# A new order table for all engines of a decoder layer: weight sums and loads at other places, the same instructions

## The chip, the core and the metric

The kernel runs on one core of one Trainium2 chip. Its time is the device time of the program in microseconds (us), the median of several runs.

## The reference

One post-norm hybrid decoder layer on 512 tokens of width 1024, all in float32. A combined input projection feeds two mixers: an attention with three branches (compressed blocks, selected blocks, sliding window) and a gated DeltaNet (a short convolution, a decay per head, a chunked recurrence). The two results are merged with gates and projected; then comes a gated MLP of width 2816 with a convolution of width 3 between the up-projection and the activation.

```python
h = x @ w_in
y_a = nsa_attention(...) @ w_nsa_out
y_b = gated_deltanet(...) @ w_gdn_out
mix = (sigmoid(gate_a) * y_a + sigmoid(gate_b) * y_b) @ w_o
x = layer_norm(ALPHA * x + mix, ln1_g, ln1_b)
f = conv_ffn(x, ffn_w_up, ffn_conv_w, ffn_w_down)   # up, conv, silu(gate) * val, down
x = layer_norm(ALPHA * x + f, ln2_g, ln2_b)
```

## The kernel before

**Arithmetic.** TensorE works on float32 values that are cut into two halves: a cast makes the high half, a subtraction from the original the low half. For weights, `split_w` loads a raw tile by a DMA on SP's queue (three buffers `raw`), ACT casts it to `wh` (L424, three buffers) and DVE subtracts to get `wl` (L428, three buffers), each for one half of the tile at a time. `product` then runs three matmuls per slice of the contraction: high by high (L438), high by low (L440) and low by high (L441), 24 matmuls for the 8 slices of a width of 1024.

**Stages.** By the profile's clock: the input projection and the mixers up to some 340 us; the merge with its gates (tiles `pm` and `gps`) to about 425; the output projection (`o_product`, L1243, with its loads in `o_load`, L1126 to L1130) and the first layer norm (L1188 to L1208) to about 475; the up-projection to about 735; the down-projection (L1407) to about 847; at the end the second layer norm and the stores.

The up-projection has 22 pairs p of a gate block and a value block. A pair is two products in two PSUM tiles `pu`; ACT scales one tap of the convolution (L1362), DVE adds the other two (L1365), ACT takes the tanh, and Pool (GpSimd) multiplies gate and value (`fth`, L1371). ACT casts this to `ph` and DVE makes the low half and the sums of blocks that the down-projection needs. Each engine executes its instructions in their order, so ACT's casts of activations (`ph`) and of weights (`wh`, L424) stand in one line.

**Sums of weights.** The output projection and the down-projection are each done with 7 products of blocks in place of 8, as in Strassen's scheme. That needs sums of weight blocks, which are made in DRAM by Pool's DMA queue, partly with accumulation: four tiles `osum` (L458, 8 DMAs of 1024 KB) and four tiles `wsum` (L468, 8 DMAs of 2816 KB). `wsum` is made by `sums(n, after)` in the up-projection, at the pairs in `ROUNDS`; two of its DMAs copy an earlier sum into a new tile before more is added:

```python
todo = [[(0, w_block(0, 0), 0), (1, w_block(0, 1), 0)], [(0, w_block(0, 1), 1)], [(1, w_block(1, 1), 1)],
        [(2, wsum[1], 0)], [(2, w_block(0, 0), 1)], [(3, wsum[2], 0)], [(3, w_block(1, 0), 1)]][n]
for to, src, add in todo:
    i = G.dma_start(out=wsum[to], in_=src, **({"accum_op": OP.add} if add else {}))
```

The down-projection's `block` (L1331 to L1343) and `o_load` read these sums as they read the weights themselves.

**Decays.** Near the start DVE makes the decay factors of the DeltaNet: `gdec` (L576), 16 values a row, then two halves of it, and PE multiplies it by three constant matrices into `dps` (L582). At the same time ACT, Pool and DVE work on the taps of the short convolution (L598 on Pool, L600 on DVE).

**The order.** `body` emits all instructions; then `queues()` chains the instructions of each engine in an order written out by hand in the table `QUEUES`. A number there is the place of an instruction in the order in which the engine's instructions were emitted, and the engine executes them in the order of the table. It holds 3880 numbers for PE, 1275 for DVE, 799 for ACT, 172 for Pool and 185 for SP. The numbers that matter below:

- Pool: 104 to 111 are the eight DMAs of `osum`. 140 and 141 are the copies that begin `wsum0` and `wsum1`; 144 and 147 add to them; 150 copies `wsum1` to `wsum2` and 153 adds to it; 157 copies `wsum2` to `wsum3` and 160 adds to it. 112 and those after are the small works of merge, first norm and up-projection, among them the 22 products `fth`. 3 is the addition of a tap of the convolution.
- SP: 76 loads the rows of the first layer norm (`ln1`, L1188), 77 to 80 are the loads of x, 81 to 89 loads of the output projection, 90 to 93 the first loads of the up-projection (`raw<-in_up`), 135 loads the rows of the second norm.
- DVE: 54 is `gdec`, 74 a tap of the convolution (L600); 833 is the first statistic of the first norm (L1250), 876 the subtraction for the first weights of the up-projection (L1301).
- PE: 2558 to 3790 is most of the up-projection and the down-projection.

```python
for n in range(int(a), int(b or a) + 1):
    i = made[k][n]
    if last is not None:
        tc.add_manual_dep(i, last.name, mybir.DependencyInfo(
            mybir.DependencyClass.NoSync, mybir.DependencyReason.SCHED_ONLY), reason="place in its queue")
    last = i
```

Of the kernel before, what the change touches and what calls it, by code (L numbers as in the profile page):

```python
# [14 lines left out]
OP = mybir.AluOpType  # L15
# [5 lines left out]
KD = 8  # L21
# [49 lines left out]
def layout(a):  # L71
# [58 lines left out]
SUMS = [4, 5, 2, 3, 8, 9, 10, 22]  # L130
# [4 lines left out]
    "PE": """0-9 11-12 10 13-39 47 40-43 53 44-45 54 50 46 48-49 59 51 60 55-56 52 57-58 61 65 62 66 63-64 74 71 75 67-69 72-73  # L135
77-78 83 76 79 84 86-87 85 70 95 89-91 80-81 107 88 108 98 82 109-112 99 92 101 96 113-118 102 97 93 103 119-120 94
121-123 100 124-149 155-172 150 173-178 151-154 104-106 183-204 207 205-206 208-230 235-236 179-181 237 182 238-247
259 248-249 260 250-252 261-262 253 263 254-255 231 264 256 265-267 232-234 257 268-269 302 270 258 271 303 272-277
304 278 305 279-281 306 282 307 360-361 308-311 283-298 362-363 388 364-367 389 368-371 390 372-377 391 378 312-313
379 392 380-382 393 383 394 299-301 314-315 395-410 416 411 444 417-418 445-446 419-433 456 434 457-458 435 459 436  # L140
447 437 460-462 448-449 463 438-439 464-471 450 472-474 451 316 320 317-318 321 319 322-323 475-477 324-327 513 478
514 328 332-334 329-331 335-339 515 479 516 340-347 517-518 348-355 519-520 356-359 384-387 521-524 412-413 525-527
414 528-529 415 530-532 440-443 533 723-730 480-481 452 534 484 482-483 731-732 485 501-502 733 535 734 486 453 735
487 536 736 503 454 488 504 489 737 490 455 738 751 491-492 739-742 493 752 494 743 495 505 507-508 744 506 496-497
753-756 745 509 757-758 541 510 542 759-760 511-512 498 761-762 543 499 763 546 544-545 547 746 764-765 500 766 548
767 560-561 549-551 768-772 552 773 562 774 565 563 553 566 554-555 567-569 537-538 591 539 556-557 592 564 540 581
558 570 582 593-597 559 598-600 796 571 797-799 583-584 800 585 801-802 586 572 803-804 573-574 805-806 575-576
587-589 601 807 602 808-809 577 810-811 590 603-604 578-579 605 812-813 651 606-607 814 652 580 815-816 608-611 653
620 817 621 654 612 818-819 622-626 613-617 864-865 618-619 627 641-642 628-629 866-868 630 869-871 643 872-873
# [12 lines left out]
968 1238 1150 1239 1151 969 1152 1179 1153-1154 1237 970-971 1155 1180 1156-1157 972-973 1181 1158 1182 1240-1241 974
1159 975 1160 976 1161 1183 1162-1164 1184-1189 1242 1190-1193 1243 1194-1199 1025 1137-1140 1026-1027 1200-1201 1283
1028 1284-1285 1202 1244 1286 1252-1253 1287 1307 1165-1168 1308 1245 1169 1309-1310 1170 1311 1254 1257 1312-1314
1246 1258 1247 1255 1259 1171-1173 1260 1174 1256 1315 1175 1316-1317 1261 1176 1248-1249 1262 1177-1178 1273-1274
1318 1288 1319 1250-1251 1275 1277 1289-1290 1263 1278 1291 1264-1267 1276 1320-1322 1268 1323 1279 1403-1404
1269-1271 1229 1324-1325 1280-1281 1272 1326 1282 1327 1230 1292 1328-1329 1405 1330 1406 1293 1407-1408 1231 1294
1409-1413 1295 1232 1296-1298 1422 1299-1302 1414 1303 1423 1415-1416 1424-1425 1417 1426 1418 1427 1379 1428
1304-1305 1380-1382 1419-1420 1383-1385 1429-1430 1386 1431 1443 1432 1444 1387-1392 1445 1331 1421 1306 1447-1448
1433-1434 1446 1435-1437 1449 1438-1440 1393 1441 1453-1454 1450 1332 1442 1394-1395 1455-1456 1396 1458 1451-1452  # L170
1459 1397 1457 1398-1401 1477 1402 1460-1461 1333-1334 1472 1478-1479 1462-1463 1473 1480-1481 1474 1482-1483 1475
1464 1484-1486 1501-1502 1465 1487-1489 1466-1467 1476 1503 1490 1468 1504-1505 1469 1506 1470 1335 1517 1471
1339-1342 1336-1338 1507-1508 1518 1509-1511 1343-1346 1512 1491 1513 1492 1347-1348 1351-1358 1349 1514 1350
1493-1498 1359-1366 1519 1521-1522 1499 1367 1371-1374 1368-1370 1523 1582 1520 1583 1544 1500 1515-1516 1375-1378
1524-1525 1584 1545 1585 1527 1610-1614 1528-1529 1526 1586-1587 1530 1546-1548 1615 1549-1550 1616 1531 1551-1553
1617 1532 1618 1554 1619 1588 1533 1589 1563-1564 1590 1620 1555 1621 1556 1534-1535 1557 1622 1591 1565 1558 1623
1592 1536 1559-1560 1568-1569 1561 1593-1594 1570-1571 1537 1566-1567 1538 1624 1562 1625-1626 1595-1598 1539 1572
1634 1627-1628 1573 1540 1635 1629-1630 1599 1541 1636 1600 1574 1637 1631 1638 1575 1632 1601-1602 1542-1543 1633
1576-1578 1603-1604 1639-1641 1579-1580 1642 1605 1581 1643-1644 1658-1659 1645-1646 1660 1647 1661-1663 1606-1608
1664-1666 1609 1648 1667-1672 1649-1650 1673-1676 1682-1683 1677 1684-1686 1678-1679 1687-1688 1680 1689 1681 1690  # L180
1651-1652 1691-1692 1653 1694 1654 1695 1655 1706 1656 1693 1707 1696 1657 1697-1698 1718-1719 1708 1699 1709 1700
1710-1713 1701-1702 1720-1722 1703 1714-1715 1723 1704 1724 1716 1705 1725-1726 1730-1731 1717 1732 1727 1733
1742-1743 1728 1744 1729 1734 1745 1735 1746-1752 1754 1753 1736 1755 1737-1739 1756 1740 1757-1758 1741 1759-1763
1778 1764-1765 1779-1788 1766-1768 1789 1769 1790 1770 1791 1771-1772 1802 1773 1792 1774 1793 1803-1804 1775-1776
1794-1795 1777 1805 1796 1806 1814 1797-1799 1807 1800 1815-1817 1808 1801 1818-1819 1809 1820 1826 1810 1821-1823
# [125 lines left out]
def body(ctx: ExitStack, tc: tile.TileContext, d, out):  # L311
    nc = tc.nc
    V, A, G, PE = nc.vector, nc.scalar, nc.gpsimd, nc.tensor
# [979 lines left out]
    first = {}  # L1293
# [233 lines left out]
```

## Time and profile before

| | |
|---|---|
| median of 3 runs | 857.27 us (855.77 to 859.29) |
| the profiled execution, time | 855.53 us |
| its span in the trace | 853.7 us |
| mean granted clock of TensorE | 0.983 |
| SP's DMA queue (q1) | 87.37 MB, 28560 packets |
| Pool's DMA queue (q0) | 31.46 MB, 8224 packets |
| DMA in all | 119.57 MB, 140 GB/s in the mean |

The span runs from the first to the last event that the profiler recorded, the time of the execution takes in what lies around it. The granted clock is the share of TensorE's full speed that the throttle allowed. The shares of busy time of the engines stand in the prediction.

### The profile page before, as it was taken

What the parts mean: (1) busy time and instruction counts of PE and PEld (TensorE: products, weight loads), DVE (VectorE), ACT (ScalarE), POOL (GpSimd) and SP (SyncE); (2) the same over time, 40 slices, a digit from 0 to 9 for tenths busy, and PEclk for the clock granted to TensorE, in tenths of its full rate; (3) what the DMA queues carried; (4) which work ended last, traced back from release to release, by engine and by line L of the source; (5) the groups of instructions that cost most, each with busy time, mean ns of one, the idle gap of its engine ahead of it and who ended that gap; (6) DMA issues with size and microseconds to landing.
All of it is one profiled execution on the core that took longest, in us unless ns stands there. A gap on an engine that the chain in (4) does not pass through costs nothing.

```text
span 853.7 us, 11766 instructions
## 1 busy us (share of the span) xinstructions
PE 814.2 (95%) x4138; PEld 674.5 (79%) x4138; DVE 616.5 (72%) x1339; ACT 409.5 (48%) x912; POOL 178.5 (21%) x176
## 2 busy tenths in 40 slices
PE   9799999899999999999998999979689999999996
PEld 8688788778788888888786988868568888887884
DVE  5757779979868965575578948747287777767886
ACT  4434477864567764232353324424144444556541
POOL 0334634232075111331100102122021111100000
PEclk9999999999999999999999999989989999999998
DMA  8423160052114033343266212989897932475662
GB/s 275 137 82 102 51 170 29 25 144 95 60 51 99 26 81 93 124 148 124 76 205 237 75 50 97 349 177 277 196 211 242 225 99 87 135 254 168 200 229 99
DMA packets 36842, 119.57 MB, mean 140 GB/s; under 512 B 3472, under 2 KB 4624, under 8 KB 35600
## 3 DMA queue, kind: packets, MB, share of 16 engines
q1 hardware_dynamic: 28560, 87.37, 31.6%
q0 software_dynamic: 8224, 31.46, 15.5%
q8 instruction: 32, 0.52, 0.2%
q14 instruction: 26, 0.21, 0.1%
HBM read 116.72 MB, written 33.55 MB: 176 GB/s over the span
## 4 chain that ended last, share of the span: by engine, by line
PE 74%; DVE 11%; issue 7%; DMA 4%; ACT 2%; POOL 2%; SPq 0%; DVEq 0%; POOLq 0%; ACTq 0%
PE gps L438 8%; PE gps L440 8%; PE gps L441 8%; PE pu L441 7%; PE pu L438 6%; PE pu L440 6%; PE px L1407 5%; PE pz L1407 3%; PE pout L1044 2%; PE pm L438 2%; PE pm L441 2%; PE pm L440 2%; PE aps L1030 2%; PE dps L614 1%; DVE wl L428 1%
## 5 line engine op out<-in xcount | busy, mean ns | idle before, releaser
L428 DVE TENSOR_TENSOR wl<-raw,wh 128x512 fp32r<-128x512 f32 x146 | 112.8, 774 | 59.6 <-ACT wh L424 46.0
L438 PE MATMUL pu<-mh,wh 128*128 128x512 f32 (+1 forms) x384 | 141.0, 379 | 12.7 <-ACT wh L424 12.7
L441 PE MATMUL pu<-mh,wl 128*128 128x512 f32 (+1 forms) x384 | 141.2, 379 | 1.3 <-DVE wl L428 1.3
L440 PE MATMUL pu<-ml,wh 128*128 128x512 f32 (+1 forms) x384 | 140.8, 377 | 0.0
L424 ACT ACTIVATE wh<-raw 128x512 fp32r<-128x512 f32 x126 | 78.7, 627 | 116.8 <-PE pu L440 79.0
L438 PE MATMUL gps<-xh,wh 128*128 128x512 f32 x320 | 126.8, 406 | 1.8 <-ACT mt L1076 1.8
L441 PE MATMUL gps<-xh,wl 128*128 128x512 f32 x320 | 126.7, 409 | 0.6 <-DVE wl L428 0.6
L440 PE MATMUL gps<-xl,wh 128*128 128x512 f32 x320 | 127.0, 405 | 0.0
L438 PEld LDWEIGHTS pu<-mh,wh 128*128 128x128 f32 x384 | 72.4, 191 | 26.5 <-ACT wh L424 13.6
L441 PEld LDWEIGHTS pu<-mh,wl 128*128 128x128 f32 x384 | 72.7, 191 | 15.3 <-DVE wl L428 2.4
L440 PEld LDWEIGHTS pu<-ml,wh 128*128 128x128 f32 x384 | 72.5, 192 | 13.0 <-DVE ml L1223 0.2
L1365 DVE SCALAR_TENSOR_TENSOR fa<-pu,fcw,fa 128x511 f32<-128x511 f32 (+1 forms) x88 | 65.5, 746 | 12.1 <-ACT fa L1362 10.7
L438 PEld LDWEIGHTS gps<-xh,wh 128*128 128x128 f32 x320 | 60.8, 191 | 12.9 <-issue 2.6
L441 PEld LDWEIGHTS gps<-xh,wl 128*128 128x128 f32 x320 | 60.7, 190 | 11.7 <-DVE wl L428 0.7
L440 PEld LDWEIGHTS gps<-xl,wh 128*128 128x128 f32 x320 | 60.7, 190 | 10.1
L1371 POOL TENSOR_TENSOR fth<-fth,fa 128x512 f32<-128x512 f32 x22 | 32.6, 1484 | 155.0 <-DVE fa L1365 132.9
L1342 ACT ACTIVATE wh<-raw 128x512 fp32r<-128x512 f32 x67 | 40.3, 626 | 40.4 <-DMA raw<-in_down 9.5
L1343 DVE TENSOR_TENSOR wl<-raw,wh 128x512 fp32r<-128x512 f32 x67 | 43.7, 684 | 19.5 <-ACT wh L1342 19.5
L480 POOL TENSOR_TENSOR rs<-rs,minus_half 128x1 f32<-128x1 f32 x8 | 7.2, 899 | 173.9 <-DVE rs L1201 173.9
L428 POOL TENSOR_TENSOR wl<-raw,wh 128x512 fp32r<-128x512 f32 x30 | 39.5, 1320 | 13.8 <-PE gps L441 6.5
L1003 ACT ACTIVATE sc<-sc,mn 128x384 f32<-128x384 f32 (+2 forms) x64 | 35.6, 558 | 13.6 <-DVE mn L1001 12.4
L1030 PE MATMUL aps<-ident,sc 128*128 128x128 f32 x160 | 35.1, 276 | 1.2 <-DVE sc L1014 0.7
(365 smaller groups left out, 1722.8 us busy)
## 6 DMA issues: line engine op xcount, KB each, us to landing
raw<-in_up SPq DMA_DIRECT2D x44, 512.0 KB, 5.4
raw<-in_wT SPq DMA_DIRECT2D x40, 512.0 KB, 3.6
wsum<-in_down POOLq DMA_DIRECT2D x6, 2816.0 KB, 21.8
raw<-wsum SPq DMA_DIRECT2D x20, 512.0 KB, 3.9
raw<-in_down SPq DMA_DIRECT2D x15, 512.0 KB, 4.0
osum<-in_wo POOLq DMA_DIRECT2D x6, 1024.0 KB, 8.4
wsum<-wsum POOLq DMA_DIRECT2D x2, 2816.0 KB, 11.5
raw<-in_wm SPq DMA_DIRECT2D x8, 512.0 KB, 3.8
```

What stands on the lines that cost most here:

```text
L424: A.activation(wh, r, AF.Copy)
L428: eng.tensor_tensor(wl, r, wh.bitcast(F32), op=OP.subtract)
L438: i = PE.matmul(ps, wh[k], mh_(k), start=(k == 0), stop=False)
L440: PE.matmul(ps, wh[k], ml_(k), start=False, stop=False)
L441: PE.matmul(ps, wl[k], mh_(k), start=False, stop=(k == n - 1))
L1003: A.activation(s[:, i, :n], s[:, i, :n], AF.Exp, scale=-1.0, bias=mn[:, 0, i:i + 1], accum_out=mn[:, 1, i:i + 1])
L1030: PE.transpose(pt[:, i, k, :], s[:, i, k * 128:(k + 1) * 128], ident)
L1342: A.activation(hi, raw[:, i], AF.Copy)
L1343: V.tensor_tensor(lo, raw[:, i], hi.bitcast(F32), op=OP.subtract)
L1365: V.scalar_tensor_tensor(acc[:, n:], ps[:, :S - n], w[:, i:i + 1], acc[:, n:], op0=OP.mult, op1=OP.add)
L1371: G.tensor_tensor(th, th, g[1], op=OP.mult)
L1407: m = PE.matmul(ps, a[x][:, j, ts], w[y], start=first and i == 0, stop=last and i == 2, skip_group_check=True)
```

## The change

Every table of `QUEUES` is replaced by a permutation of itself. The instructions, their buffers, their bytes and their engines are the same. `SUMS` and `FIRST`, which had no effect any more, are removed. So many instructions stand at another place in their engine's order, with the largest shift: 3372 of 3880 on PE (79 places), 1111 of 1275 on DVE (152), 640 of 799 on ACT (23), 145 of 172 on Pool (73), 55 of 185 on SP (13).

The whole of Pool's and SP's tables:

```diff
-    "Pool": """2 1 0 8 10 9 105 11 3-4 12-13 5-7 15-17 19-22 18 27-28 33 36 34 25 23 29 39 30-31 14 32 40 107 43 35 24 108 44 41 26
-37 54-55 45 48 51 42 49 47 62 52 66 92 67-68 104 46 69 109 65 64 57 50 58 53 56 110 59 38 61 63 80 60 87 81 75 90
-76-78 84 71-72 85 73 70 86 94 74 93 82 106 89 91 95 88 79 96-97 83 98-100 111 101-103 112-138 142 139 143 141 145 140
-147 146 148 150 149 151 144 153 152 154-155 157 156 158 160 159 161-171""",
-    "SP": """0-7 17 8-9 15 25 10 18 11-14 19 16 20-23 26-33 24 34-75 79 77-78 81-82 80 83-90 76 91-134 136-141 135 142-165 167 169
-171 173-174 166 168 175 170 172 176-184""",
+    "Pool": """2 1 0 8 10 9 3 12 11 104 15 13 16 4 105 5-7 17 19 107 20-21 106 22 27-28 33 108 38 25 23 34 29 39 30 18 31-32 40 43-44
+35 14 24 109 41 45 54-55 36 26 110 48 51 42 49 47 52 111 65-67 64 62 68 46 92 57-58 69 37 50 56 59 61 53 63 75 77 90
+80 60 76 81 78 84 86-87 71 85 72-73 70 94 74 93 82 91 95-96 79 83 98 88-89 97 99-103 141 112-114 116 115 117-132 140
+133-137 147 138-139 142 150 143 145 148 146 149 153 151-152 154-155 157 144 156 158-163 165 164 166-171""",
+    "SP": """0-7 17 8-9 15 25 10 12 11 13-14 19-21 16 18 22-23 26-28 24 29-75 81-82 79-80 83 78 77 76 84-134 136-154 135 155-165
+167 169 171 173-180 170 168 172 166 182 181 183-184""",
```

On PE the up-projection and the down-projection, which stood in the order of emission, are now interleaved; the new rows begin like this and go on in the same manner:

```diff
-2497 2509 2481 2510 2498 2511 2499 2512 2500-2502 2513-2515 2503-2504 2516-2519 2505 2520-2521 2530-2532 2522-2525
-2533 2526-2527 2534 2528-2529 2535-2539 2554 2540 2555-2556 2541 2557 2542-2553 2558-3790 3793 3791-3792 3794-3796
...
+2544-2545 2554-2555 2546 2528 2547 2529 2548-2550 2556 2551 2557 2552 2558-2559 2553 2560-2564 2578 2565-2569 2579
+2570-2572 2580 2573 2581-2584 2574 2585-2589 2575-2577 2590-2591 2602-2604 2592 2605-2610 2593 2611-2612 2594
```

On DVE `74 53-54 68-71` near the start becomes `53 90 54 74`, and `876 833` in the output projection becomes `833 876`. ACT's rows change by small shifts all over. The code beside the tables:

```diff
-SUMS = [4, 5, 2, 3, 8, 9, 10, 22]
...
-    FIRST = {}
...
-        for (to, src, add), u in zip(todo, SUMS):
-            i = G.dma_start(out=osum[to], in_=src, **({"accum_op": OP.add} if add else {}))
+        for to, src, add in todo:
+            G.dma_start(out=osum[to], in_=src, **({"accum_op": OP.add} if add else {}))
...
-        FIRST[u] = first = product(ps, w, (lambda k: xh[:, k, :], lambda k: xl[:, k, :]), KD)
+        first = product(ps, w, (lambda k: xh[:, k, :], lambda k: xl[:, k, :]), KD)
```

More of the change, by code (lines that the diff above doesn't have):

```diff
@@ L140 @@
[L140 to L149, printed above, removed]
@@ new lines @@
+1155-1156 974 1157-1159 1181 975 1241 976 1160-1161 1182 1162-1164 1183-1190 1252 1191-1193 1254 1242 1025 1137 1243
+1255 1138 1256 1139-1140 1194 1253 1195-1198 1244 1199 1283 1245 1200-1202 1284 1257 1026-1028 1246 1258 1307 1285
+1308 1286 1165-1168 1247 1309-1311 1169-1170 1312-1314 1287 1259-1261 1171-1172 1262 1273 1315-1317 1274 1248
+1173-1174 1275 1249 1175 1250 1176-1177 1251 1178 1277 1318 1263-1264 1319 1265 1278 1266 1288 1267 1279 1276 1280
+1268-1270 1403 1289-1290 1404 1271 1291-1293 1320-1324 1229 1281 1405 1282 1406 1408-1409 1272 1325-1326 1230
@@ new lines @@
+1327-1330 1294 1410 1407 1411-1413 1231 1295-1300 1422 1301-1302 1423 1303 1414 1232 1424-1427 1304 1415 1379 1428
+1416-1417 1380 1305 1381-1385 1306 1429 1418 1443-1444 1386-1387 1430-1431 1445 1432 1388-1389 1419 1447 1420-1421
+1448 1477 1390-1393 1433 1394 1434-1439 1446 1449-1450 1440 1453-1454 1395 1478 1441-1442 1479-1480 1396 1481 1331
+1455-1456 1451-1452 1458-1459 1397 1482 1398-1399 1483 1460 1457 1332-1333 1461 1472 1462-1463 1400-1401 1473
+1484-1485 1402 1486-1488 1474-1476 1501 1582 1502 1464 1489-1490 1583 1465-1467 1334 1503-1505 1468 1506 1335 1469
@@ new lines @@
+1517-1518 1339 1336 1470 1340 1337 1471 1341-1342 1338 1491-1492 1507-1508 1493 1343-1346 1519 1521 1509 1494-1495
+1510 1347-1349 1522 1350-1358 1520 1496-1499 1511 1359-1366 1523 1512-1514 1584-1585 1500 1367-1374 1524 1544-1545
+1525 1375-1378 1526 1586 1515 1610 1546 1527 1547 1549 1611 1516 1612 1528 1548 1587-1588 1529-1530 1550 1589-1590
+1613 1531-1532 1551-1553 1614 1591 1615 1563-1564 1616 1592 1617 1593 1618 1554 1533-1534 1565 1594 1619 1595 1620
+1535 1621 1596 1555 1622 1556 1623 1536 1566 1568 1537 1569 1557 1597-1598 1538-1539 1567 1558-1559 1599-1601
@@ new lines @@
+1734 1742 1735 1743-1744 1736 1745-1747 1729 1748 1737 1749 1754 1750 1755 1751 1738 1752 1756 1739-1740 1757 1753
+1758-1760 1741 1761-1763 1778 1764-1766 1779 1767-1769 1780 1770 1781 1771 1782-1785 1772-1775 1786-1790 1776-1777
+1791-1793 1802-1805 1794-1795 1806-1809 1796 1810-1812 1797 1813-1818 1798-1799 1826 1819-1820 1800 1821-1823 1801
+1824-1825 1827-1840 1850-1851 1841-1842 1852 1843-1844 1853-1854 1845 1855 1846 1856-1858 1847 1859-1861 1848
+1862-1864 1874-1875 1865 1876-1880 1849 1881 1866-1867 1882 1868 1883 1869 1886 1884 1870 1885 1887-1890 1898
@@ new lines @@
+1891-1895 1871 1899 1896 1900-1901 1872 1902 1873 1903-1905 1897 1906-1920 1922-1926 1921 1946 1927-1929 1947
+1930-1931 1948-1949 1932 1950 1933 1951-1952 1934-1935 1958 1953 1959-1961 1954 1962 1955-1956 1963 1957 1964-1969
+1936-1945 1970-2004 2018 2005-2008 2030 2019 2009-2012 2020-2021 2031 2013 2022 2014 2032 2023-2024 2015 2025
+2016-2017 2026 2033-2034 2027 2035-2036 2042 2028-2029 2037-2038 2043-2044 2039-2040 2054 2045-2047 2041 2055-2056
+2048 2057-2061 2049-2050 2062-2063 2051-2053 2064-2066 2069 2067 2070 2068 2071-2072 2093 2090-2091 2094 2075-2076
@@ new lines @@
+2613-2615 2595 2616-2617 2596 2626-2628 2618 2629 2597 2619-2622 2630-2631 2598 2623 2599-2600 2624 2601 2632-2633
+2625 2634-2635 2650 2636-2637 2651 2638-2644 2652-2660 2645 2661-2662 2646-2647 2674 2663-2669 2648 2670 2649
+2675-2679 2671-2672 2680 2673 2681-2685 2698 2686-2687 2699-2700 2688-2690 2701-2705 2691 2706-2708 2692 2709 2693
+2710 2694 2711 2722-2724 2695-2696 2725 2712 2697 2726 2713-2715 2727-2731 2716 2732 2717 2733-2734 2718-2719
+2735-2736 2746 2737-2738 2747 2720-2721 2748 2739-2741 2749-2755 2742-2743 2756-2757 2744 2758 2745 2759-2760 2770
@@ new lines @@
+2911 2938 2929 2939 2930 2912 2940 2931-2933 2941-2946 2913 2947-2950 2934-2936 2951-2952 2962-2963 2953 2964 2937
+2965 2954 2966-2972 2955-2956 2973 2957-2959 2986 2960-2961 2987 2974 2988 2975 2989 2976 2990 2977 2991-2993 2978
+2994-2995 2979-2981 2996 2982-2984 2997-3004 3010 3005-3006 3011 2985 3012 3007-3009 3013-3016 3034 3017 3035
+3018-3019 3036-3039 3020-3021 3040-3042 3022-3027 3043 3028 3044 3029-3030 3045 3031-3032 3058 3046-3048 3059-3061
+3033 3062-3063 3049-3051 3064-3067 3052 3068 3053-3055 3069 3056 3070 3082-3083 3057 3071-3072 3084 3073-3075
@@ new lines @@
+3250-3252 3240 3253-3255 3225 3241-3244 3256-3269 3245 3270 3246 3271 3247 3274-3275 3272 3248-3249 3273 3276-3279
+3298 3280-3283 3299-3300 3284-3285 3301 3286 3302 3287-3288 3303-3304 3289 3305-3306 3290 3307-3308 3291-3293
+3309-3310 3322 3294 3311-3313 3323-3325 3314 3326-3327 3315 3328 3295-3297 3329-3333 3316-3319 3346 3334 3347-3348
+3335 3349-3350 3320 3336 3351-3353 3337 3354 3338-3341 3355 3321 3342-3343 3356-3358 3344 3359-3361 3345 3370-3371
+3362 3372 3363 3373-3374 3364-3369 3375-3379 3394 3380-3382 3395 3383 3396-3397 3384-3385 3398 3386-3387 3399
@@ new lines @@
+3645 3649-3651 3655-3656 3646-3648 3652-3654 3658 3657 3661 3659 3662-3663 3667 3660 3664-3665 3668-3669 3673 3666
+3674-3675 3685 3670-3671 3682 3672 3686 3683 3679 3676 3684 3687 3677 3691 3688 3692 3680 3678 3689-3690 3693 3697
+3694-3695 3698 3696 3700 3699 3703 3681 3701-3702 3704 3706-3707 3705 3709 3708 3712 3710-3711 3713-3714 3718 3715
+3719-3720 3716-3717 3724 3721 3725-3726 3730 3722-3723 3727-3729 3731-3732 3736 3733 3748 3737 3734 3738 3735
+3742-3743 3739-3741 3744-3745 3751-3752 3746 3753 3747 3749-3750 3757 3754-3756 3760-3762 3758-3759 3763-3765
@@ new lines @@
+3769-3770 3766-3767 3771 3768 3772 3775-3777 3773 3781 3774 3782-3783 3787-3788 3778-3780 3784-3786 3789-3791
+3793-3794 3792 3795-3798 3802-3804 3799 3805-3807 3800-3801 3808-3818 3847 3819-3822 3848 3823 3849-3858 3824 3859
+3825 3860 3826 3861 3827-3846 3862-3879""",
+    "DVE": """0 27 104 1-4 6 5 7 9 8 11 10 12-15 17 16 18-19 58-61 64 20 65 23 66 26 67 62 21-22 63 31-32 72 33-39 29 73 40-44 30
+45-50 115 51-53 90 54 74 68-69 91 55 25 285 83 70-71 56 81 84 92 82 102 85-86 93 87 94 88 80 95 75 151 153 152 76 154
```

267 lines of the change are left out of this document (136 added, 131 removed), and 4 rows, old and new, of the table QUEUES.

## The prediction

> **What bounds the kernel now.** I read the page first, then the busy time in stretches of 25 us, then PE's and Pool's waits, then Pool's timeline where PE stood still.
>
> ```profile
> span 853.7 us, 11766 instructions
> PE 814.2 (95%) x4138; PEld 674.5 (79%) x4138; DVE 616.5 (72%) x1339; ACT 409.5 (48%) x912; POOL 178.5 (21%) x176
> ...
> 25.00:50.00 25.00, 20.70 (x81) 16.63 (x80) 15.36 (x37) 8.95 (x22) 8.15 (x9) 0.86 0.32 106
> ...
> 375.00:400.00 25.00, 25.00 (x110) 20.38 (x109) 16.21 (x27) 7.31 (x14) 7.60 (x8) 1.00 0.40 122
> ...
> 550.00:575.00 25.00, 20.41 (x76) 15.96 (x76) 12.55 (x21) 7.93 (x15) 4.62 (x3) 0.86 0.84 214
> 575.00:600.00 25.00, 25.00 (x112) 20.68 (x111) 18.05 (x28) 10.21 (x18) 5.13 (x4) 1.00 0.98 272
> 600.00:625.00 25.00, 15.60 (x61) 12.07 (x60) 7.89 (x13) 4.61 (x8) 3.63 (x3) 0.83 0.86 179
> 625.00:650.00 25.00, 25.00 (x108) 20.56 (x108) 18.95 (x28) 11.78 (x21) 4.12 (x4) 0.97 1.01 286
> ```
>
> The columns are the stretch, then busy time (and instructions) of PE, weight loads, DVE, ACT and Pool, the granted clock, the DMA share and GB/s. TensorE is busy 95%: it is the bound, and only its holes can be gained. In the up-projection an undisturbed stretch does 112 matmuls in 25 us, 0.223 us each. Two stretches do 76 and 61 and a third 108, and the clock is down to 0.86 and 0.83 in the first two. 36 + 51 + 4 = 91 matmuls are missing: 91 x 0.223 = 20.3 us, the largest hole of the trace.
>
> ```profile
> PE pu L438 <- ACT wh L424: 12.7, 2, 9.0
> PE dps L582 <- issue: 4.3, 1, 4.3
> PE pw L1243 <- DVE mv L1199: 3.2, 1, 3.2
> ...
> 540.75 1.06 POOL L468 DMA_DIRECT2D wsum<-in_down  x1
> 560.07 1.76 POOL L468 DMA_DIRECT2D wsum<-in_down  x1 [18.26 <-issue]
> 560.98 2.14 POOL L1371 TENSOR_TENSOR fth<-fth,fa 128x512 f32<-128x512 f32 x1
> ...
> 581.86 0.55 POOL L468 DMA_DIRECT2D wsum<-wsum  x1 [12.77 <-DMA wsum<-in_down]
> ...
> 590.35 1.76 POOL L468 DMA_DIRECT2D wsum<-in_down  x1
> 616.97 1.71 POOL L468 DMA_DIRECT2D wsum<-in_down  x1 [24.86 <-issue]
> ...
> 676.21 1.29 POOL L1371 TENSOR_TENSOR fth<-fth,fa 128x512 f32<-128x512 f32 x1 [9.58 <-DVE fa L1365]
> ```
>
> First PE's waits (total, times, longest), then Pool's timeline (start, duration, idle time before). Pool issued an accumulating weight sum directly behind another large copy and stood for 18.26 and 24.86 us. The activation product (L1371) queued behind it; ACT's cast of that product (ph) stood in front of ACT's cast of the next weights (wh), and PE waited for those: 3.7 and 9.0 us, and the half clock after. A Pool delay of 12.77 us, before 581.86, cost PE nothing: 575:600 has its full 112.
>
> **The change part by part.** Instructions and bytes stay, so the sum starts from the profiled execution, 855.53 us (span 853.7).
>
> ```profile
> wsum<-in_down POOLq DMA_DIRECT2D x6, 2816.0 KB, 21.8
> ...
> wsum<-wsum POOLq DMA_DIRECT2D x2, 2816.0 KB, 11.5
> ```
>
> Weight sums. I read the new Pool table by its numbers. 141 goes ahead of the merge stage's first cast, 140 to the end of that stage, 147 behind the last rs of the first norm, 150, 153 and 160 behind the products of pairs 2, 7 and 14; 157 with 144 right behind it stands after pair 11. A pair takes 1.29 + 9.58 = 10.9 us of Pool. A copy from in_down lands in 21.8 us: from 147 to 150 are three products and the stretch before them, 150 to 153 five (54 us), 153 to 157 four (43 us), 144 to 160 three (33 us). None of these then waits. Behind a wsum-to-wsum copy the trace issues without a hold: the DMA at 590.35 has no idle time before it and came 8.5 us after the copy at 581.86, inside its 11.5 us. So no issue holds Pool beyond its own 0.55 to 1.76 us, inside 9.58 us of idle time. I take the whole 20.3 us off; what is late next is PE's own rate. Of the osum copies, issued earlier now, none stood in PE's way before, nor does one now: nothing.
>
> ```profile
> L576 DVE SCALAR_TENSOR_TENSOR gdec<-sacc,ea x1: 3193/3193/3193, 37.0 to 37.0; 128x16 f32<-128x16 f32 x1
> ...
> 38.83 2.62 POOL L598 TENSOR_TENSOR acc<-acc,tap 128x510 f32<-128x510 f32 x2
> ```
>
> Decays. PE stood 4.3 us (its waits, above) for gdec, which took 3.19 us for 16 elements a row, beside Pool operations without a pause. In the new DVE table gdec (54) comes ahead of a convolution tap (74), and on Pool a tap's addition (3) moves ahead of a copy. Bounds: nothing, or the wait and the clock, 4.3 + (1 - 0.86) x 25 = 7.8 us. I take 3.0, gdec's own excess, since Pool's two-input operations stay near it.
>
> ```profile
> 455.47 0.42 SPq L1188 DMA_DIRECT2D ln<-in_lnr  x1
> ...
> 455.09 6.50 DMA raw<-in_up
> ```
>
> Output projection. The first in_up load took 6.50 us with the 1 MB ln load right behind it; DVE stood for it, with the additions that free PE's banks queued behind. The new SP table issues ln (76) six loads earlier, and DVE does one statistic (833) before that split. Bounds: 0 to 3.2 us; I take 2.9, from 6.50 to the 3.6 of an undisturbed load (below).
>
> The next rows are the landing of the in_up loads issued from 480 to 530 us (no sum in flight) and from 533 to 560 us (sums in flight).
>
> ```profile
> DMA to landing us min/median/max: 3.4/3.6/4.1
> ...
> DMA to landing us min/median/max: 6.3/8.1/9.0
> ```
>
> Collisions, a cost. A weight load takes 3.6 us alone and 8.1 beside a sum. 141 and 140 now fly during the merge stage and the head of the output projection, where loads have less time in hand than in the up-projection. SP's order of the weight loads is nearly unchanged. Bounds: none (575:600 did 112 matmuls beside sums, the DMA engines at 0.98), or one late load each, 2 x 4.5 = 9 us. I take 2.0, near the row that lost nothing.
>
> Interleaved products, a cost. Before, a product's 24 matmuls ran as one block (2558-3790); now two products alternate almost to the end of the down-projection (2578 between 2564 and 2565, and so on). Counting in the table, the half of a weight tile that takes over a freed buffer is first needed 5 or 6 matmuls later in 18 of some 120 cases, against 24 as a rule before. The merge stage alternates already, with handovers of 5 matmuls, and did 110 in 25 us against 112. Bounds over 300 us: nothing, or 2/112 of it, 5.4 us; I take 2.0, since the merge stage's row holds waits of its own.
>
> The merge row also has the granted clock at 1.00. The Trainium skill (TensorE: Matmul & The Clock Gate, section "A second HAM failure mode: psum-queue depth-cycling") says that a kernel cycling through PSUM banks can idle PE for moments so often that its clock keeps falling to half; by that rule the new order would lose the clock again and again in the up- and down-projection, and the time would come out above that of before, where the merge row would leave it below. The trace of before does not bear it out; as a rival it stands below.
>
> The mixers (50 to 340 us) are re-ordered throughout; I found no wait that plainly goes or comes, and put nothing.
>
> Sum: 855.5 - 20.3 - 3.0 - 2.9 + 2.0 + 2.0 = 833.3. The median of the runs, 857.27, is 1.74 above the profiled execution, so the forecast is 835.0.
>
> **The rivals.**
> - The block comes back elsewhere: 144 behind 157 holds Pool as the second stall did. For it: both were issues directly behind a copy in flight. Against: 590.35, above. One stall of 51 matmuls, 11.4 us: 846.
> - It does not pay: the loads become the bound. Counted in the table, the time from a raw buffer's release to the need of its next content shrinks from 58 matmuls (13 us) to about 44 (10 us), at the least 28, and a load beside a sum takes 8.1, with cast and subtraction after it. About 18 up loads fly beside a sum; if each is 1.3 us late, 23 us come back: 835.0 - 2.0 + 23 = 856, no change. Against: a delay of PE gives the loads in flight as much more time, and 10 us is still more than 8.1 with a cast.
> - Slower: the handovers. If each of the 120 halves waits for half of one ACT cast in front of it,
>
> ```profile
> L424 ACT ACTIVATE wh<-raw 128x512 fp32r<-128x512 f32 x126 | 78.7, 627 | 116.8 <-PE pu L440 79.0
> ```
>
> 0.31 us, PE loses 38 us in the up- and down-projection: 835.0 - 2.0 + 38 = 871. It decides from (857.3 - 835.0 + 2.0 + 4.3) / 120 = 0.24 us a handover, 4.3 us (0.5%) above the time before. For it: PE, ACT and DVE are in-order and the slack is cut to a fifth. Against: the merge stage.
> - Slower by the clock (the page's rule, above): one fall in each of twelve stretches, (1 - 0.86) x 25 = 3.5 us each, is 42 us: 877. Against: 1.00 in the merge row.
>
> **How the numbers follow.** Forecast 0.79, the returned block 0.07, no change 0.07, slower 0.06 by the handovers and 0.01 by the clock. Range: down to 855.5 - 20.3 - 7.8 - 3.2 = 824, up to 855.5 - 20.3 + 9 + 5.4 = 850, which takes in the returned block. A measurement of this kernel can tell about 0.5%, 4.3 us, from no change. Faster by more: 0.79 + 0.07 = 0.86; within: 0.07; slower: 0.07.
>
> **What would show it.** Right: no Pool wait at L468 of over 3 us, fth evenly 10.9 us apart, 110 or more matmuls in every 25 us of the up-projection with the clock at 1.00; PE's wait at L582 under 2 us and at L1243 under 1 us; new waits of ACT wh for DMA raw below 4 us in all. Wrong: a Pool wait behind 157; the up-projection at 105 matmuls or fewer with waits of PE for wh L424 spread over it (handovers), or of ACT wh for DMA raw (loads); a span over 848.

## The result, and the profile after

The changed kernel takes 834.4 us (median of 4 runs, 832.38 to 834.61) against 856.94 us of the kernel before (4 runs, 855.77 to 859.29): a ratio of 0.9728, 95% interval 0.9703 to 0.9754. The ratios of the experiments below are each against executions of the kernel before that were made beside them; their medians lie between 854.5 and 856.8 us. The span of the profiled execution of the changed kernel is 832.2 us, 21.5 us below 853.7. The same line of code has a number that is 39 or 40 higher than before (`product` L478 to L481, the copies into wsum L507).

The page of the changed kernel, and its busy time in stretches of 25 us (columns as in the prediction):

```profile
span 832.2 us, 11752 instructions
PE 807.3 (97%) x4138; PEld 671.6 (81%) x4138; DVE 604.6 (73%) x1339; ACT 408.2 (49%) x912; POOL 177.8 (21%) x176
...
25.00:50.00 25.00, 22.67 (x102) 18.03 (x100) 18.23 (x51) 12.05 (x30) 13.03 (x14) 1.00 0.38 129
...
325.00:350.00 25.00, 23.13 (x99) 18.55 (x97) 14.01 (x21) 11.36 (x20) 1.72 (x2) 0.93 0.61 200
...
400.00:425.00 25.00, 22.41 (x91) 17.79 (x90) 13.11 (x23) 7.23 (x17) 4.76 (x5) 0.93 0.66 229
...
550.00:575.00 25.00, 25.00 (x112) 20.65 (x110) 18.76 (x31) 10.55 (x19) 3.92 (x4) 1.00 0.29 94
575.00:600.00 25.00, 25.00 (x112) 20.71 (x111) 15.70 (x24) 10.27 (x18) 4.59 (x4) 1.00 0.96 219
600.00:625.00 25.00, 25.00 (x112) 20.72 (x111) 17.71 (x29) 11.40 (x21) 4.19 (x4) 1.00 0.31 101
625.00:650.00 25.00, 22.34 (x99) 18.18 (x98) 14.82 (x24) 8.31 (x14) 1.98 (x2) 1.00 1.00 263
```

The two stretches with 76 and 61 matmuls are gone, and 25:50 does 102 in place of 81. But there are three new holes, two in the merge stage (99 and 91 matmuls, clock 0.93) and one at 625:650 (99). The kernel before did more in the first two stretches, at a clock of 1.00:

```profile
325.00:350.00 25.00, 25.00 (x121) 20.82 (x120) 17.15 (x30) 12.36 (x25) 2.84 (x2) 1.00 0.27 85
400.00:425.00 25.00, 23.23 (x103) 18.91 (x102) 13.25 (x23) 6.43 (x13) 4.17 (x4) 1.00 0.23 75
```

PE's longest waits, and Pool's timeline around the place where 144 stands right behind 157:

```profile
PE pm L478 <- ACT wh L464: 4.5, 2, 2.6
PE pu L478 <- ACT wh L464: 2.9, 2, 2.7
PE gps L478 <- DVE kl L906: 1.5, 1, 1.5
```

```profile
622.11 1.29 POOL L1410 TENSOR_TENSOR fth<-fth,fa 128x512 f32<-128x512 f32 x1 [8.29 <-DVE fth L1409]
623.35 0.55 POOL L507 DMA_DIRECT2D wsum<-wsum  x1
623.88 1.78 POOL L507 DMA_DIRECT2D wsum<-in_down  x1
632.68 1.31 POOL L1410 TENSOR_TENSOR fth<-fth,fa 128x512 f32<-128x512 f32 x1 [7.02 <-DVE fth L1409]
```

The waits for gdec (L582 before) and for the first norm (L1243 before) no longer stand among them, and neither copy holds Pool. The new holes start at ACT, which waits for a load. Two rows, from the waits between 400 and 425 us and from those between 620 and 650:

```profile
ACT wh L464 <- DMA raw<-in_wm: 4.5, 1, 4.5
```

```profile
ACT wh L464 <- DMA raw<-in_up: 5.0, 1, 5.0
```

To add this up by stage I take for each matmul the time to the start of the next one, less the lower quartile of that time among all matmuls of the same operands and shape in the twelve traces of this study. The sum is what PE lost, the half clock included. The stages are cut at the first matmul into pm, the first and the last into pw, and the first into px. In us:

| kernel | mixers | merge | output projection | up | down | span |
|---|---|---|---|---|---|---|
| before | 60.2 | 2.5 | 4.6 | 23.1 | 2.5 | 853.7 |
| after | 53.0 | 8.8 | 1.3 | 7.1 | 0.9 | 832.2 |
| sums only (old order) | 59.0 | 10.2 | 6.1 | 2.8 | 4.1 | 843.0 |
| sums back (new order) | 53.6 | 0.4 | 1.2 | 32.2 | 2.1 | 850.6 |
| sums early (new order) | 54.4 | 0.4 | 1.3 | 3.6 | 1.1 | 821.9 |
| sums early and spaced (old order) | 67.1 | 3.4 | 3.0 | 2.9 | 1.9 | 839.2 |

From before to after that is -7.1 + 6.3 - 3.3 - 16.0 - 1.6 = -21.7, and 0.3 comes back behind the last matmul (8.27 us before, 8.55 after). The expectations below were written with fewer traces at hand; their sums differ from the table by up to 0.4 us in the up-projection and 3 in the mixers.

### The profile page after: what moved, and what is told of

It reads as the page before. It is cut to its first block, busy times and chain, and to the rows that moved or that the text cites. A ratio compares the mean times of both kernels' runs of the same rounds, so it can differ in the third digit from the quotient of the medians.

```text
span 832.2 us, 11752 instructions
## 1 busy us (share of the span) xinstructions
PE 807.3 (97%) x4138; PEld 671.6 (81%) x4138; DVE 604.6 (73%) x1339; ACT 408.2 (49%) x912; POOL 177.8 (21%) x176
## 4 chain that ended last, share of the span: by engine, by line
PE 82%; DVE 7%; DMA 7%; ACT 2%; issue 1%; POOL 1%; SPq 0%; DVEq 0%; ACTq 0%; POOLq 0%
PE pu L478 9%; PE pu L480 9%; PE pu L481 9%; PE gps L478 7%; PE gps L480 7%; PE gps L481 7%; PE px L1446 5%; PE pz L1446 4%; PE pw L1282 3%; PE pout L1083 2%; PE pu L1282 2%; PE aps L1069 2%; PE pm L478 2%; DMA raw<-in_up 2%; PE pu L1446 2%; PE pm L480 2%
## 5 line engine op out<-in xcount | busy, mean ns | idle before, releaser
L468 DVE TENSOR_TENSOR wl<-raw,wh 128x512 fp32r<-128x512 f32 x146 | 107.3, 739 | 81.9 <-ACT wh L464 53.6
L478 PE MATMUL pu<-mh,wh 128*128 128x512 f32 (+1 forms) x384 | 131.0, 373 | 3.3 <-ACT wh L464 2.9
L480 PE MATMUL pu<-ml,wh 128*128 128x512 f32 (+1 forms) x384 | 130.8, 372 | 0.0
L481 PE MATMUL pu<-mh,wl 128*128 128x512 f32 (+1 forms) x384 | 130.4, 372 | 0.0
L478 PE MATMUL gps<-xh,wh 128*128 128x512 f32 x320 | 125.6, 402 | 2.5 <-DVE kl L906 1.5
L481 PE MATMUL gps<-xh,wl 128*128 128x512 f32 x320 | 125.3, 401 | 0.0
L480 PE MATMUL gps<-xl,wh 128*128 128x512 f32 x320 | 125.0, 399 | 0.0
L478 PEld LDWEIGHTS pu<-mh,wh 128*128 128x128 f32 x384 | 71.3, 188 | 17.2 <-ACT wh L464 3.8
L481 PEld LDWEIGHTS pu<-mh,wl 128*128 128x128 f32 x384 | 71.2, 188 | 12.8
L480 PEld LDWEIGHTS pu<-ml,wh 128*128 128x128 f32 x384 | 71.0, 188 | 12.3
L1410 POOL TENSOR_TENSOR fth<-fth,fa 128x512 f32<-128x512 f32 x22 | 30.6, 1399 | 211.6 <-DVE fth L1409 169.2
L478 PEld LDWEIGHTS gps<-xh,wh 128*128 128x128 f32 x320 | 60.3, 189 | 15.5 <-issue 3.4
L480 PEld LDWEIGHTS gps<-xl,wh 128*128 128x128 f32 x320 | 60.7, 190 | 10.9
L481 PEld LDWEIGHTS gps<-xh,wl 128*128 128x128 f32 x320 | 60.4, 189 | 10.2
L1382 DVE TENSOR_TENSOR wl<-raw,wh 128x512 fp32r<-128x512 f32 x67 | 44.0, 685 | 14.5 <-ACT wh L1381 12.3
L1401 ACT ACTIVATE fa<-pu,fcw 128x512 f32<-128x512 f32 x44 | 29.6, 679 | 29.5 <-PE pu L481 26.9
L468 POOL TENSOR_TENSOR wl<-raw,wh 128x512 fp32r<-128x512 f32 x30 | 39.4, 1318 | 20.3 <-ACT wh L464 10.7
L1042 ACT ACTIVATE sc<-sc,mn 128x384 f32<-128x384 f32 (+2 forms) x64 | 35.7, 560 | 11.5 <-DVE mn L1040 11.4
## 6 DMA issues: line engine op xcount, KB each, us to landing
wsum<-in_down POOLq DMA_DIRECT2D x6, 2816.0 KB, 22.5
```

Source lines behind the costliest of these rows:

```text
L468: eng.tensor_tensor(wl, r, wh.bitcast(F32), op=OP.subtract)
L478: i = PE.matmul(ps, wh[k], mh_(k), start=(k == 0), stop=False)
L480: PE.matmul(ps, wh[k], ml_(k), start=False, stop=False)
L481: PE.matmul(ps, wl[k], mh_(k), start=False, stop=(k == n - 1))
L1042: A.activation(s[:, i, :n], s[:, i, :n], AF.Exp, scale=-1.0, bias=mn[:, 0, i:i + 1], accum_out=mn[:, 1, i:i + 1])
L1382: V.tensor_tensor(lo, raw[:, i], hi.bitcast(F32), op=OP.subtract)
```

## The experiments

Theory 1: the places of the sums in Pool's table made the gain, by ending Pool's holds, and made the price, by loads that come late beside a sum in flight. Theory 2: the new order of PE, DVE and ACT made the gain.

**Only the sums moved, in the kernel before.** Pool's table from its 113th place:

```diff
-112-138 142 139 143 141 145 140 147 146 148 150 149 151 144 153 152 154-155 157 156 158 160 159 161-171
+141 112-132 140 133-137 147 138 142 139 150 143 145-146 148-149 153 151-152 154-155 157 144 156 158-171
```

> The kernel before, with nothing changed but the places of the eight wsum copies in Pool's table: they stand at the places of the changed kernel (141 behind 103, 140 behind 132, 147 behind 137, 150 behind the third product, 153 behind the eighth, 157 and 144 behind the twelfth, 160 behind the fifteenth). PE, DVE, ACT and SP keep the old order. Theory 1 (Pool's blocked issue was the loss, the order of the other engines gives next to nothing in the up-projection): no Pool wait at the copies above 3 us; what PE loses in the up-projection falls from 22.8 to some 7 us, what it loses in the merge stage rises from 2.5 to some 9 us, as in the changed kernel; time 847 us (844 to 850). Theory 2 (the new order of PE, ACT and DVE carries the gain): PE still loses 12 us or more in the up-projection, time 852 us or more.

Measured: 846.14 us, ratio 0.9887 (0.9860 to 0.9915). The up-projection loses 2.8 us in place of 23.1: the 20.3 us of the forecast, by Pool's table alone. The merge loses 10.2 in place of 2.5. Theory 1 holds for the stalls. But the time fell by only 10.7 us (from 856.79 of the kernel before beside it), less than half of the 22.5 us of the whole change: the rest came with the other moves. The up-projection is even better than in the changed kernel (7.1), with the same copies in flight:

```profile
621.70 0.56 POOL L468 DMA_DIRECT2D wsum<-wsum  x1
622.24 1.77 POOL L468 DMA_DIRECT2D wsum<-in_down  x1
```

```profile
625.00:650.00 25.00, 25.00 (x112) 20.71 (x111) 17.06 (x28) 10.38 (x18) 2.87 (x2) 1.00 1.04 277
```

First Pool's timeline, then the busy time. In both kernels the in_up load issued right behind 144 is the slowest, 13.8 us here and 14.5 in the changed kernel. The old order covers it (112 matmuls), the new order does not (99). That it re-uses the raw buffers sooner is the likely reason; PE's order was not run apart from that of ACT and DVE, so this is argued and not shown.

**The sums put back, in the changed kernel.** Pool's table from its 113th place, the rest as changed:

```diff
-141 112-114 116 115 117-132 140 133-137 147 138-139 142 150 143 145 148 146 149 153 151-152 154-155 157 144 156 158-163
+112-114 116 115 117-139 142-143 141 145 140 147-148 146 150 149 151 144 153 152 154-155 157 156 158 160 159 161-163
```

> The changed kernel, with nothing changed but Pool's table behind the mixers: the wsum copies stand again where they stood before (141 and 140 behind the fourth and fifth product, 147 directly behind 140, 144 and 153 together behind the ninth). Theory 1: Pool is held 15 to 25 us at 147 and at 153, PE loses 12 to 20 us more in the up-projection, and gets back the 6 us that it loses in the merge stage: 844 us (840 to 850). Theory 2 (the interleaved order of PE, ACT and DVE covers such a hold): 838 us or less.

Measured: 852.15 us, ratio 0.9950 (0.9930 to 0.9970), 2 us above the range. The merge is clean (0.4), the up-projection loses 32.2 us. Pool's timeline and PE's waits:

```profile
552.60 1.76 POOL L507 DMA_DIRECT2D wsum<-in_down  x1 [14.12 <-DVE fa L1404]
...
575.87 0.56 POOL L507 DMA_DIRECT2D wsum<-wsum  x1 [18.95 <-DMA wsum<-in_down]
...
617.48 1.71 POOL L507 DMA_DIRECT2D wsum<-in_down  x1 [21.80 <-issue]
```

```profile
PE pu L481 <- DVE wl L468: 22.6, 2, 12.7
```

The first row is 147. The view names DVE, but 147 came 0.46 us behind the landing of 140 (552.14), and this wait of 14.12 us cost PE nothing: between 550 and 570 us it did 92 matmuls in 20 us. PE's two waits fall in the other two rows: 9.9 us while 150 waited for the landing of 147, which it copies, and 12.7 us while 153 was held. There DVE's subtraction for the next weights stands behind the work that waits for Pool. So the new order covers one of the three waits of Pool and pays more for the other two than the old order did. As a cover for holds theory 2 fails; part of the gain is still the new order's, since this kernel is 4.6 us below the kernel before (856.79).

**All sums in the mixers, in the changed kernel.** Pool's table: 141 behind 111, 147 behind 92, 150 behind 59, 153 behind 53, 157 behind 86, 140 behind 70, and at the end of the mixers

```diff
-98 88-89 97 99-103 141 112-114
+98 88-89 97 144 99 160 100-103 112-114
```

> The changed kernel, with all eight wsum copies moved in Pool's table into the mixers (from 148 to 272 us), 160 directly behind 144 where Pool has no work for 35 us. Theory 1 with late loads as the price of a sum in flight: PE's waits for wh at 340, 415 and 639 us (2.0, 2.8 and 2.8 us, with the clock 3.4, 4.7 and 3.0) go, the merge stage loses 2.5 us and the up-projection some 3 us: 824 us, if the loads of in_wT have enough time in hand in the mixers; each that has not costs up to 4.5 us, so 822 to 835. Rival: these three waits have another cause than the sums (ACT's order) and stay, then 834 us or more. On the hold: 160, an accumulating copy directly behind an accumulating copy in flight, holds Pool for 15 us or more if room for the copies is what Pool waits for.

Measured: 824.43 us (823.97 to 825.28), ratio 0.9625 (0.9610 to 0.9639): 10.0 us below the changed kernel, and the fastest version of this study. The three late waits for wh are gone, the merge loses 0.4 us and the up-projection 3.6; the mixers pay 1.4 us. The busy time, and Pool's timeline where 160 stands behind 144:

```profile
400.00:425.00 25.00, 25.00 (x111) 20.39 (x110) 16.27 (x29) 9.03 (x20) 2.49 (x3) 1.00 0.56 182
...
625.00:650.00 25.00, 25.00 (x112) 20.70 (x111) 16.89 (x28) 10.50 (x18) 3.14 (x2) 1.00 0.30 93
```

```profile
272.33 1.81 POOL L507 DMA_DIRECT2D wsum<-in_down  x1
293.79 1.72 POOL L507 DMA_DIRECT2D wsum<-in_down  x1 [18.32 <-issue]
```

The hold is there, 18.32 us, and costs nothing, since Pool had no work until 307 us in the changed kernel. That the late loads were the sums' doing is seen in their landing, over the loads of raw between 320 and 430 us, in the changed kernel and then here:

```profile
DMA to landing us min/median/max: 3.2/3.8/9.1
```

```profile
DMA to landing us min/median/max: 3.3/3.6/4.6
```

**Three sums moved, in the changed kernel.** 141 behind 111, 140 behind 99, and 144 two products later:

```diff
-157 144 156 158-163
+157 156 158 144 159-163
```

> The changed kernel, with three copies moved in Pool's table: 141 directly behind 111 (147 us), 140 behind the last subtraction of the mixers (272 us), 144 from behind 157 to behind the next product but one. Late loads as the price: the three waits of PE for wh in the merge stage and at 639 us go, 834.4 - 3.4 - 4.7 - 3.0 = 823 us, up to 828 with one or two late loads elsewhere. Rival (ACT's order, not the sums): the waits stay within 1 us of where they are, 833 us or more.

Measured: 827.74 us, ratio 0.9663 (0.9643 to 0.9683). In the range, but not for the reason alone: in the traced execution (829.91 us, the slowest of the four) the merge is clean (0.3), while the up-projection loses 11.4 us in place of 7.1. Pool's timeline, then DVE's:

```profile
642.56 1.73 POOL L507 DMA_DIRECT2D wsum<-in_down  x1
652.64 1.30 POOL L1410 TENSOR_TENSOR fth<-fth,fa 128x512 f32<-128x512 f32 x1 [8.35 <-DVE fth L1409]
666.93 1.74 POOL L507 DMA_DIRECT2D wsum<-in_down  x1 [12.99 <-DVE fa L1404]
667.84 3.34 POOL L1410 TENSOR_TENSOR fth<-fth,fa 128x512 f32<-128x512 f32 x2
```

```profile
667.36 4.38 DVE L468 TENSOR_TENSOR wl<-raw,wh 128x512 fp32r<-128x512 f32 x1 [0.69 <-ACT wh L464]
674.63 0.69 DVE L468 TENSOR_TENSOR wl<-raw,wh 128x512 fp32r<-128x512 f32 x1 [2.89 <-PE pu L481]
```

Moving 144 brought it within 24 us of 160, and 160 is held 12.99 us, until 144 landed at 666.59. Then two products ran on Pool without a pause, and DVE's subtraction beside them took 4.38 us instead of 0.69.

**More room for descriptors, in the kernel before.** What does Pool wait for? Not for data at the end: in the trace of before 147 was held to 560.07, though the copy that it adds to (141) had landed at 548.05; the other copy, 140, landed at 559.60.

```diff
-    nc = bacc.Bacc("TRN2", target_bir_lowering=False, num_devices=1, dynamic_dma_scratch_size=4096)
+    nc = bacc.Bacc("TRN2", target_bir_lowering=False, num_devices=1, dynamic_dma_scratch_size=4864)
```

> The kernel before, with one number changed: the memory kept for the descriptors of Pool's DMAs is 4864 bytes a partition instead of 4096 (more does not fit beside the kernel's tiles). Theory A (Pool waits for room for descriptors, and an accumulating copy takes about twice the room of a plain one): 147, behind one plain copy in flight, is issued when the semaphore that it needs comes (the landing of 141, some 12 us earlier than before), so its hold falls from 18 to some 6 us and PE's first stall (3.9 us, with the clock 8) mostly goes; 153, behind an accumulating copy, may stay held to that copy's landing. Some 849 us. Theory B (an accumulating copy waits for a copy from in_down in flight for another reason than room): both holds end 0.3 to 0.5 us behind the landing of the copy before, as now; 857 us.

Measured: 855.61 us in its one run, with 855.85 for the median of before beside it. Pool's timeline:

```profile
552.28 1.78 POOL L468 DMA_DIRECT2D wsum<-in_down  x1 [8.15 <-DMA wsum<-in_down]
...
615.90 1.71 POOL L468 DMA_DIRECT2D wsum<-in_down  x1 [24.17 <-issue]
```

Theory A holds for 147: it is now held 8.15 us, released by the copy that it adds to (landed at 551.66) and not by 140, which is in flight until 562.08; PE loses nothing between 550 and 575. 153, behind an accumulating copy, is held as before; whether it too waits for room is not shown. The expected time was not reached: the second stall and places elsewhere lost more, the output projection 7.8 us in place of 4.6 among them. That was one run, and why is open.

**The small moves, in the kernel before, in two pairs.** First SP's 76 and DVE's 53 and 54:

```diff
-SP: 80 83-90 76 91-134
+SP: 80 83 76 84-134
-DVE: 74 53-54 68-71
+DVE: 53-54 74 68-71
```

> The kernel before with two small moves, at places far apart. On SP the load of the first norm's rows (76) goes six loads earlier, behind 83: if the late in_up load is the cause of the stall in the output projection, PE's wait of 3.2 us at L1243 falls below 1 us and that load lands in some 4 us; if DVE's order is the cause, the wait stays at 3 us. On DVE gdec and the instruction before it (53, 54) go ahead of the tap 74: if the place in DVE's table sets the stall at L582, gdec takes some 0.4 us instead of 3.19 and PE's wait of 4.3 us falls below 1.5; if Pool's order beside it is the cause, gdec still takes 2 us or more. Both gains together: 849 us; none: 857.

Measured: 851.74 us (one run), gdec at 1.29 us, PE's wait for it no longer among the first rows. The first in_up load landed in 4.14 us (6.50 before), and the wait at L1243 fell to 1.3. Both causes are confirmed in part. Then their counterparts:

```diff
-DVE: 876 833
+DVE: 833 876
-Pool: 9 105 11 3-4
+Pool: 9 3 105 11 4
```

> The kernel before with the two counterparts. On DVE the statistic 833 goes ahead of the subtraction 876 that waits for the first in_up load: if DVE's order is the cause of the stall in the output projection, PE's wait of 3.2 us at L1243 falls below 1 although the load stays late (6.5 us). On Pool the addition of a tap (3) goes ahead of the first osum copy (105) and of a subtraction: if Pool's order is the cause of the long gdec, it takes less than 1 us and PE's wait at L582 falls below 2 us; else both stay as they are. Both: 849 us; none: 857.

Measured: 847.76 us (one run). The wait at L1243 stayed at 2.8: DVE's order is not the cause there, and the landing of the load is: in the five traces of the old order in which it took 5.6 to 6.7 us the wait was 2.8 to 3.6 us. But gdec, in DVE's old order, took 0.175 us. The timeline of this kernel (compare 3.19 us at 37.0, in the prediction):

```profile
37.25 0.17 DVE L576 SCALAR_TENSOR_TENSOR gdec<-sacc,ea 128x16 f32<-128x16 f32 x1
37.65 1.26 POOL L598 TENSOR_TENSOR acc<-acc,tap 128x510 f32<-128x510 f32 x1 [0.46 <-ACT tap L597]
```

In the kernel before and in the run with gdec ahead of the tap, Pool was busy when gdec began:

```profile
36.84 0.75 POOL L458 DMA_DIRECT2D osum<-in_wo  x1
37.60 1.29 POOL L428 TENSOR_TENSOR wl<-raw,wh 128x512 fp32r<-128x512 f32 x1
```

```profile
36.04 1.26 POOL L428 TENSOR_TENSOR wl<-raw,wh 128x512 fp32r<-128x512 f32 x1
36.05 1.29 DVE L576 SCALAR_TENSOR_TENSOR gdec<-sacc,ea 128x16 f32<-128x16 f32 x1
```

Before, Pool issued a DMA at 36.84, ahead of gdec, and went on without a pause; with gdec ahead of the tap, gdec began beside a subtraction on Pool and ended with it; with the tap's addition moved, Pool waits 0.46 us for a tap, and gdec comes first. PE loses 5.7 us less between 25 and 50 us (1.9 against 7.6); the first pair gained 3.1 there. In the other traces of the old order this loss was 6.3 to 8.0, so both gains can be some 1 us smaller.

**All sums in the mixers, in the kernel before, two tries.** First: 141 behind 109, 147 behind 50, 150 behind 110, 153 behind 61, 157 behind 63, 140 behind 75, 144 behind 70, 160 behind 88.

> The kernel before with nothing changed but that all eight wsum copies stand in the mixers in Pool's table (160 directly behind 144 near 270 us); PE, DVE, ACT and SP keep the old order. If the sums in flight are what makes loads late and the order of the other engines is neutral in the up-projection: PE loses some 2.5 us in the merge stage, as before, and some 2.4 us in the up-projection instead of 22.8: 857 - 20.4 = 836.5 us, 833 to 842. The rest, some 12 us to the changed kernel with its sums in the mixers, would then be the order of the other engines in the mixers, the merge, the output and the down-projection. If the sums disturb the mixers of the old order, 843 or more.

Measured: 859.47 us, ratio 1.0040 (1.0017 to 1.0063): the whole gain is lost. The up-projection loses 2.8 us, as expected, but the mixers 82.2. Pool's timeline and PE's waits:

```profile
213.61 0.52 POOL L468 DMA_DIRECT2D wsum<-wsum  x1 [11.61 <-DMA wsum<-in_down]
...
289.32 1.73 POOL L468 DMA_DIRECT2D wsum<-in_down  x1 [5.78 <-issue]
```

```profile
PE dps L720 <- DVE gx L718: 14.5, 2, 8.1
```

150 stood in Pool's queue before the sum that it copies had landed. Pool's next product (db, L683) waited behind it, DVE waited for db, and PE for DVE, 8.1 us: the same loss at another place. The other 6.3 us fall in the hold of 160, behind 144, with work of the mixers (rn, L480) queued behind it. Second try, with the copies farther apart (141 behind 44, 147 behind 45, 150 behind 67, 153 behind 50, 157 behind 61, 140 behind 63, 144 behind 78, 160 behind 95):

> The kernel before with nothing changed but the places of the eight wsum copies in Pool's table: all in the mixers, as in the run before this one, but so far apart that no accumulating copy comes while a copy from in_down is in flight and none comes before the sum that it adds to has landed (141 near 117 us, 147 near 137, 150 near 168, 153 near 186, 157 near 211, 140 near 222, 144 near 242, 160 near 268). If the run before lost its gain to Pool's holds alone (two waits of PE for gx, 15 us, and the clock), these waits go: 57 to 62 us lost in the mixers, 2.5 in the merge, 2.5 in the up-projection, time 836 us (833 to 840). If copies in flight disturb the mixers of the old order by themselves: 845 or more.

Measured: 841.05 us, ratio 0.9830 (0.9801 to 0.9859), 1 us above the range. No copy is held and the two waits for gx are gone, so Pool's waits made most of the loss; 7 us more than before are still lost in the mixers (67.1 against 60.2), by what is open. With Pool's 3 and SP's 76 moved as well:

> As the run beside it, and two more moves that single runs have shown: on Pool the addition of a tap (3) ahead of the first osum copy, on SP the load of the first norm's rows (76) six loads earlier. PE, DVE and ACT keep the old order. If the parts add up: 836 - 5.7 - 1.7 = 829 us (826 to 833), so that less than 6 us are left to the changed kernel with its sums in the mixers (824.4), for the whole new order of PE, DVE and ACT. If they do not add up: 833 or more.

Measured: 834.18 us, ratio 0.9750 (0.9710 to 0.9790). By its number the run falls to the rival (833 or more), but only since the spaced sums had come out 5 us above the 836 that it starts from: the two moves gain 6.9 us against 7.4 expected. Nearly all of it is in the mixers (5.9); SP's move had little left to gain, since the first in_up load of the spaced sums landed in 4.97 us and PE's wait at L1243 was 1.6 us already. Ten moves in Pool's and SP's tables reach the time of the changed kernel (834.4), which moves thousands of instructions. Against the changed kernel with its sums in the mixers (824.4), 9.8 us are left and not the less than 6 expected; that is the worth of the rest of the new tables, most of it in the mixers.

## Why the prediction came out right

The forecast was 835.0 us and the median is 834.4; for the profiled execution it was 833.3, and that took 834.24. The largest term was right in mechanism and size. That the total came out within 1 us is luck: one cost was 10 us too small, and gains that I had not seen or had put too low made up for it.

**Weight sums, -20.3: right in mechanism and size.** The places of the sums in Pool's table alone took 20.3 us off the up-projection (23.1 to 2.8), and putting the old ones back brought more than that (7.1 to 32.2). That 144 behind 157 would not be held was right too. The reason given, a copy directly behind another large one, was too coarse: what was held was an accumulating copy behind a copy from in_down in flight (147 and 153 before and with the sums put back, 160 where 144 was still in flight), and more room ended one of these holds at the landing of the sum itself. A copy from wsum to wsum in flight held nothing (590.35 before, 623.88 after, 622.24 with the sums alone).

**Decays, -3.0: right, too small.** PE's loss between 25 and 50 us fell from 7.6 to 3.1. Of the two moves that I named, either alone shortens gdec (1.29 us by DVE's, 0.175 by Pool's). Its two inputs both lie in SBUF; the Trainium skill (SBUF — State Buffer, section "Who interferes with whom") says that such a DVE instruction and a GpSimd instruction that reads SBUF block each other, and that the order of issue decides who waits. Two runs agree: 0.17 us when gdec came 0.40 us ahead of Pool's addition, and 1.29 us when it began beside a subtraction on Pool and ended with it. The 3.19 us of before do not follow from the rule alone: gdec began at 36.95 us, behind a DMA issue on Pool but ahead of the subtraction at 37.60, and ended at 40.14, when Pool had done that subtraction and an addition more. What the issue does beside gdec was not tried alone.

**Output projection, -2.9: right (4.6 to 1.3).** The late load was the cause, as I had it, and SP's move made it land in time; the move takes the load of the rows ahead of seven loads (84 to 90), not six. SP's move with gdec's gave 1.7 of the 3.3 us (4.6 to 2.9), but this stage lost between 3.0 and 7.8 us in the traces of the old order without it, so that figure is rough. DVE's 833 alone left PE's wait as it was; what made the rest was not separated.

**Collisions, +2.0: the step that failed.** They cost 12 us: 8.4 in the merge (8.8 against 0.4 with the sums away) and 3.5 in the up-projection (7.1 against 3.6). I gave 9 us as the bound and took a value near the row that lost nothing. That row was of the up-projection, in the old order, with one copy in flight for most of it. The merge has less time in hand, as I had written: its late loads took up to 9.1 us, little more than the 8.1 that I had reckoned with, and cost PE nearly the whole bound. In the up-projection 8.1 was too little as well: the load issued right behind the first wsum-to-wsum copy, alone in flight, took 13.0 us, and the one behind the second and 144 took 14.5.

**Interleaved products, +2.0: too much.** With no sum in flight the new order loses 3.6 us in the up-projection against 2.9 in the old one, 0.7 more, and 1.1 in the down-projection against 1.9. Its cost, as far as the runs tell, is the shorter time in hand for late loads (112 against 99 matmuls beside the same copies, above), and that stood under another rival. The clock did not fall with it: a mean of 0.994 against 0.983, and 1.00 in each stretch of the up-projection above. The Trainium skill (TensorE: Matmul & The Clock Gate, section "A second HAM failure mode: psum-queue depth-cycling") tells of a clock that keeps falling in a kernel that cycles through PSUM banks; no run here shows that.

**What I put at nothing.** The mixers gained 2.6 us beyond the decays, the merge 2.1 (2.5 to 0.4 without sums in flight) and the down-projection 1.6. So 10 us too little for the collisions were made up by gains of 1.9 more in decays and norm, 1.3 that the interleaving did not cost, and 6.3 that I had not seen. What made these 6.3 was not tried.

Of the signs that I named, the products on Pool are not evenly 10.9 us apart (9.6, 10.6 and 18.1 us from 612.52 to 650.73), as two pairs now overlap; ACT's waits for loads, 4.5 us for in_wm and 5.0 for in_up, were not below 4 in all, and 625:650 had 99 matmuls, not 110: the signs of "loads", in single stretches. No wait showed behind 157.

## What to carry to other kernels

A large transfer issued from a compute engine's queue is two things to place: an instruction that can hold its engine until an earlier transfer has landed, and a load on the DMA engines that makes others late. Put it where both have room, behind the landing of what it needs and beside a stage whose loads have time in hand: here the mixers, in the changed kernel some 10 us better than the stages in which the change spread it. In the old order the same stage gave nothing until the copies stood far enough apart that none waited. When a term of the sum lies between far bounds, take the value from a row with the same time in hand and as many transfers in flight, not from the nearest clean one.

## What the runs showed of the hardware

An accumulating copy of 2816 KB was not issued while a copy from in_down of that size was in flight with 4096 bytes a partition for descriptors, and was with 4864 when that copy was a plain one (552.28 us, while 140 was in flight until 562.08). One DVE operation with two inputs took 4.38 us instead of 0.69 beside a DMA issue and two Pool products without a pause: 3.7 us lost in a single instruction. A load of 512 KB took 3.6 us with no sum in flight, up to 9.1 beside a copy from in_down in the merge, and 13.0 right behind a copy from wsum to wsum.
